# Hybrid encoder block on one core: another order of the splits of x, of the rotations and of the key loads in the in-projection

## The chip, the core and the metric

The kernel runs on one core of a Trainium2 chip. A core has TensorE (PE, matrix products into PSUM), VectorE (DVE), ScalarE (ACT), GpSimd (POOL) and SyncE (SP, which here only issues transfers), and 16 DMA engines between the device's memory and the core's on-chip memory. Each engine works through its own instructions in order; an instruction that has to wait holds up everything behind it on its engine. A transfer is issued by SP, ACT or POOL, in that engine's order, and lands later.

The metric is the time of one execution in microseconds (us) on the device. A profile shows one execution, with its span from the first to the last instruction.

## The reference

One transformer layer for a prompt of 512 tokens and a sample of 256 tokens (768 rows together), width 2048, all in float32:

```python
h = rmsnorm(x, ln_mix_g)
z = h @ w_in                      # 2048 -> 1024 Fourier | 1024 q | 256 k | 256 v
of = fourier_mix(z[..., :1024])   # 8 groups x 128 channels: Re(2-D DFT), then a 128x128 map
q, k = apply_rope(q), apply_rope(k)
oa = window_attention(q, k, v, sink)   # 16 heads, 4 key heads, +-128 positions
x = x + concat(rmsnorm(of), rmsnorm(oa)) @ w_out
x = x + relu(rmsnorm(x) @ w_up) ** 2 @ w_down
return rmsnorm(x)
```

## The kernel before

Every matrix product is made of three: each operand is split into a high part (a rounded copy, made by ScalarE) and a low part (the remainder, made by VectorE), and high x high, high x low and low x high are summed. So each weight tile and each tile of x costs one ScalarE and one VectorE instruction before TensorE can use it. The line numbers are those of the profile.

The stages in question come one after the other on TensorE:

1. **V** (L543): the value columns, chunk by chunk; x arrives transposed.
2. **Products** (`product7`, L287): six sets of columns (three column pairs, two halves of the contraction) times seven products, 42 steps, with sums of blocks of x and of the weights so that seven products serve for eight (the names a11, s1, s2, s3, a22, s4, a12). Step n issues product n on TensorE, the low part of the weights of product n+2 (L273), the sums and high part of product n+3 (L257, L265), and the load of product n+5 (L238). Two tables, `high_at` and `low_at`, say at which step a block of x is subtracted (L404), and its high (L407) and low (L410) part made; `k_at` says the same for the rotation of the keys. Beside them, rows of x are loaded again through POOL's queue (`row_load`, L613), squared by ScalarE (`row_square`, L617), summed to the row norms, transposed by TensorE (L625) into a PSUM buffer, copied by ScalarE (`row_spread`, L629, tile `rb`) and spread over the partitions. The PSUM buffer is one of two that the products also take.
3. **Pieces** (L970): twelve pieces, four for each of three pairs of query columns (pairs 2, 3 and 4), 48 matmuls each. Between them, at half and whole pieces, run the eight Fourier groups (`weights`, `fold`, `fold_parts`, `stage1`, `stage2`, `stage2_put`) and the rotations of the query pairs 1, 2 and 3, each in three thirds of 256 positions: `cross` on POOL (L336), `turned` on VectorE (L340, L342), a high part on ScalarE (L351), a low part on VectorE (L352), both stored by ScalarE's queue. What runs when is kept in a table, `todo`: key 8.5 is the middle of piece 9, key 9 its end. `piece_split` makes the two parts of the weights of a later piece; `piece_load` loads them through SP. Behind the last piece the same calls load and split the first weights of the out-projection.
4. **Out-projection and attention** (L1210, L1011): 24 slots of the out-projection, with the attention's matmuls strewn in between by a list of events in units of an eighth of a slot. The first slot needs the first Fourier rows (`load_of`, `split_of`, L1193), the first four weight pieces, queries and keys.

The order is fixed by hand: TensorE's throughout, that of SP, ACT and VectorE in the products, and those and POOL's from the pieces on; only POOL's order among the products is left to a planner that goes by its own costs.

On-chip memory is used again and again. A pool of tiles takes the place of one that was closed, and a new tile waits only for those older tiles whose place it takes. So the order in which tiles are first named in a pool decides whom they wait for; the kernel names some tiles (`name="z7"`) only to fix that order. The pool `xp` of the V stage (weights `raw`, x parts `vt`, six half-rows `xt`) gives way to `hq` of the products (tags z10, z01, d7, wr, then ws and z11), and that to `fp` of the Fourier groups. The query side has pools from the other end of the memory: `kp` (rotation) and `kq` (mask, sink, keys `kd`, queries `qs`, first Fourier rows `ofr`); `kq` can only open when `fp` is closed, at key 9.

Of the kernel before, what the change touches and what calls it, by code (L numbers as in the profile page):

```python
# [20 lines left out]
P = 128  # L21
# [19 lines left out]
def hybrid_encoder(ctx: ExitStack, tc: tile.TileContext, a: dict):  # L41
# [157 lines left out]
    with ExitStack() as ph:  # L199
# [235 lines left out]
        def first_split(e):  # L435
            for i in range(4):
                k = 4 * e + i
                split(fx["h11"][:, k], fx["l11"][:, k], fx["d"][:, i], g0[:, k : k + 1])
# [6 lines left out]
        for e in range(2):  # L445
# [5 lines left out]
            step(low_at, 12 + 2 * e, lambda e=e: difference(e))  # L451
            step(high_at, 13 + 2 * e, lambda e=e: xhigh(h1, fx["d"], e))
            step(low_at, 13 + 2 * e, lambda e=e: xlow(l1, fx["d"], h1, e))
            step(low_at, 16 + e, lambda e=e: xsum(b11, b21, b11, e))
            step(high_at, 18 + e, lambda e=e: xhigh(h0, b11, e))
            step(low_at, 19 + e, lambda e=e: xlow(l0, b11, h0, e))
            step(high_at, 24 + e, lambda e=e: xhigh(h1, b22, e))
            step(low_at, 24 + e, lambda e=e: xlow(l1, b22, h1, e))
            if e == 0:
                step(high_at, 26, second_block)  # L460
# [4 lines left out]
        step(low_at, 33, first_block)  # L465
        step(low_at, 27, lambda: first_load(0))
        for e in range(2):
            step(low_at, 33 + 4 * e, lambda e=e: first_split(e))
            if e == 0:
                step(low_at, 33, lambda: first_load(1))  # L470
# [183 lines left out]
        with tc.tile_pool(name="hq", bufs=1, reuse_waits="tile") as hq["p"], tc.manual_schedule(  # L654
            engines={mybir.EngineType.SP, mybir.EngineType.Activation, mybir.EngineType.DVE}
        ):
            for tag, shape, bufs in (("z10", [P, HALF], 3), ("z01", [P, HALF], NS7), ("d7", [P, 4, HALF], 1), ("wr", [P, 4, 256], 3)):
                hq["p"].tile(shape, F32, tag=tag, name="z7", bufs=bufs)
# [7 lines left out]
            step(k_at, 28, k_tables)  # L666
            step(k_at, 33, k_loads)
            step(k_at, 34, k_scale)
            step(k_at, 34, k_keep)
            for n in range(NP7):  # L670
# [16 lines left out]
                if n in (18, 20, 22, 24):  # L687
                    for i in range(3 * n // 2 - 15, 3 * n // 2 - 12):
                        row_square(i)
                if n in (16, 18, 20, 22):  # L690
                    for i in range(3 * n // 2 - 12, 3 * n // 2 - 9):
                        row_load(i)
                if n in (33, 34, 35):
                    back7(n - 33)
                if n == 24:
                    row_norms()
# [10 lines left out]
            for n in range(NP7, NP7 + 2):  # L707
                for fn in k_at.get(n, ()):
                    fn()
# [4 lines left out]
        fctx = ExitStack()  # L714
        fp = fctx.enter_context(tc.tile_pool(name="fp", bufs=1, reuse_waits="tile"))
        cc = fp.tile([P, 2, P], F32, tag="cc", name="cc")
# [8 lines left out]
        for tag, w, bufs in (("wf", P, 2), ("zf", T, 2), ("fe", 320, 1), ("fo", 256, 1)):  # L725
            fp.tile([P, w], F32, tag=tag, name="z7", bufs=bufs)
        fp.tile([P, 2, 2, P], F32R, tag="cw", name="cw", bufs=2)
        for tag in ("ah", "al"):
            fp.tile([P, T], F32, tag=tag, name="z7")
        tabh = fp.tile([P, 4, 256], F32R, tag="tabh", name="tabh")  # L730
        tabl = fp.tile([P, 4, 256], F32R, tag="tabl", name="tabl")


        def weights(g):
            wf = fst[g].pop("w")
            pc = pp.tile([P, 512], F32, tag="f", bufs=4, name="pc")
            cw = fst[g]["cw"] = fp.tile([P, 2, 2, P], F32R, tag="cw", name="cw", bufs=2)
# [27 lines left out]
        def fold_parts(g):  # L765
            sh = fst[g]["sh"] = fp.tile([P, 6, P], F32R, tag="sh", name="sh")
            sl = fst[g]["sl"] = fp.tile([P, 6, P], F32R, tag="sl", name="sl")
            split(sh[:], sl[:], fst[g].pop("s")[:])

        def stage1(g, b):  # L770
            if b == 0:
                for x in ("ah", "al"):
                    fst[g][x] = fp.tile([P, 6, P], F32R, tag=x, name=x)
            sh, sl, cw, ah, al = (fst[g][x] for x in ("sh", "sl", "cw", "ah", "al"))
            pa = pp.tile([P, 512], F32, tag="f", bufs=4, name="pa")
            if b == 0:
# [4 lines left out]
                t = fp.tile([P, 2, P], F32, tag="ft", name="ft")  # L781
# [21 lines left out]
        def stage2(g):  # L803
# [7 lines left out]
            of = fp.tile([P, T], F32, tag="of", name="of")  # L811
# [7 lines left out]
            else:  # L819
                sq = fst[g + 2 if g + 2 < FG else g]["z"]  # L820
# [26 lines left out]
        def open_attention():  # L847
            open_pool("kq", ("mask", [P, 384], a["c_mask"]), ("sink", [P, 64], a["attn_sink"].partition_broadcast(P)))
            kt["kd"] = kt["kq"].tile([P, NKV, T], F32R, tag="kd", name="kd")
            for u in range(3):  # L850
# [27 lines left out]
        def load_k():  # L878
            nc.sync.dma_start(f32(kt["kd"][:]), kr_d[:].rearrange("(p h) t -> p h t", h=NKV))

# [3 lines left out]
        def q_tile(u):  # L884
            state[u] = {"qs": kt["kq"].tile([P, 2, 4, P], F32R, tag="qs", name="qs", bufs=3)}
# [13 lines left out]
        def after(piece, fn):  # L899
            todo.setdefault(piece, []).append(fn)  # L900
# [3 lines left out]
        def turn(pair, s, t):  # L904
            turned(pair, s)
            parts(pair, s, lambda dt, fn: todo.setdefault(t + dt, []).insert(0, fn), (0.5, 1))
# [3 lines left out]

        def close_fourier():
            fctx.close()
            open_attention()
            load_k()

        turns = [(1, s, t) for s, t in enumerate((1, 3, 5))] + [(2, s, t) for s, t in enumerate((7, 8, 8.5))] + [(3, s, t) for s, t in enumerate((9, 9.5, 10))]
        for g in range(FG + 2):
            if g < FG:
                after(g - 0.5, lambda g=g: (weights(g), fold(g)))
            if g >= 2:  # L920
                after(g - 0.5, lambda g=g: stage2(g - 2))
            if 1 <= g <= FG:
                after(g - 0.5, lambda g=g: (stage1(g - 1, 0), stage1(g - 1, 1)))
                after(g, lambda g=g: stage1(g - 1, 2))
            if g < FG:
                after(g, lambda g=g: fold_parts(g))
            if g >= 2:
                after(g, lambda g=g: stage2_put(g - 2))
            if g + 2 < FG:
                after(g, lambda g=g: load_group(g + 2))  # L930
        for pair, s, t in turns:
            after(t - 0.5, lambda pair=pair, s=s: cross(pair, s))
            after(t, lambda pair=pair, s=s, t=t: turn(pair, s, t))
        after(9, close_fourier)
        after(9.5, fourier_norm)
        after(9.5, lambda: load_q(0))
        after(9.5, lambda: load_of(0, [kt["kq"].tile([P, 4, P], F32, tag="ofr", name="ofr", bufs=2) for _ in range(2)]))
        after(9.5, lambda: load_q(2))
        after(10.5, negate_sink)
        after(10.5, lambda: load_q(1))  # L940
# [4 lines left out]
        tabs = [fp.tile([P, T], F32, tag=t, name="tab")[:, :512].rearrange("p (k t) -> p k t", k=2) for t in ("ah", "al")]  # L945
# [1044 lines left out]
```

## Time and profile before

| | |
|---|---|
| three runs | 2588.67, 2588.93, 2590.66 us; median 2588.93 |
| the profiled execution | 2589.08 us, span 2587.3 us |
| mean granted TensorE clock | 0.995 |
| V stage on TensorE | to 40.7 us |
| products | 40.7 to 225.5 us |
| pieces | 225.5 to about 364 us |
| first out-projection matmul | 377.06 us |
| MLP and end | from about 730 us to the end |

In the rows of the profile, a time in us since the span's start comes first, then a duration, the engine, the line of the kernel, the operation, written tile <- read tiles, the shape; in brackets how long the engine sat idle before and what ended that. The list of waits has engine, line and what it waited for, then us in total, times, longest. The rows of transfers have their size and the us from issue to landing. "xN" stands for N instructions put into one row, or N in a group.

### The profile page before, as it was taken

The page shows a single profiled execution, that of the slowest core. Times are in us where ns is not written, and L with a number is a line of the kernel's source. Part 1 is how long each engine was busy: PE and PEld are TensorE (multiplying, and loading weights), DVE is VectorE, ACT ScalarE, POOL GpSimd, SP SyncE. Part 2 cuts the span into 40 slices and gives each one's busy share as a digit, 9 for nine tenths or more (in the row PEclk, how much of TensorE's full clock was granted, in tenths as well). Part 3 has the DMA queues.
Part 4 walks back from the last instruction along what each step waited for, and adds up shares of the span by engine and source line. Part 5 has one row for each costly group of instructions (what it writes and reads, how often), then busy time and mean ns, then how long its engine had stood idle before and what let it go on. Part 6 is the DMA issues. An engine that isn't in the chain of part 4 may idle for free.

```text
span 2587.3 us, 34692 instructions
## 1 busy us (share of the span) xinstructions
PE 2558.9 (99%) x13415; PEld 2341.8 (91%) x13415; DVE 1809.0 (70%) x2152; ACT 1125.9 (44%) x1622; POOL 266.8 (10%) x385
## 2 busy tenths in 40 slices
PE   9999989999999999999999999999999999999998
PEld 9989978888899999999999999988888888888887
DVE  7776757777555656555877877667776765777687
ACT  7353537774333333333444554433333333333335
POOL 0022332232201011000000000110000000000000
PEclk9999989999999999999999999999999999999999
DMA  8576367555654445456666666775543662555264
GB/s 300 201 263 222 121 193 218 149 151 193 225 190 157 163 160 188 159 190 237 213 214 232 231 214 208 245 305 176 184 155 110 218 233 82 179 179 164 97 208 155
DMA packets 260724, 496.99 MB, mean 192 GB/s; under 512 B 21098, under 2 KB 145520, under 8 KB 260304
## 3 DMA queue, kind: packets, MB, share of 16 engines
q1 hardware_dynamic: 190816, 328.20, 39.6%
q10 hardware_dynamic: 54000, 105.75, 10.9%
q0 software_dynamic: 15744, 60.83, 6.9%
q8 instruction: 105, 1.72, 0.3%
q14 instruction: 59, 0.48, 0.1%
HBM read 373.19 MB, written 121.51 MB: 191 GB/s over the span
## 4 chain that ended last, share of the span: by engine, by line
PE 94%; issue 2%; DVE 2%; ACT 1%; DMA 1%; POOL 0%; ACTq 0%; SPq 0%; DVEq 0%; POOLq 0%
PE pu L1357 36%; PE pd L1792 35%; PE pm L1210 10%; PE p L287 4%; PE pz L970 3%; PE pv L543 1%; PE s L1011 1%; PE o L1088 1%; PE t L1066 1%; PE ptx L138 0%; PE pa L789 0%; PE pe L810 0%; PE pm L1212 0%; DMA d<-in_x_sample 0%; ACT xs L407 0%
## 5 line engine op out<-in xcount | busy, mean ns | idle before, releaser
L1357 PE MATMUL pu<-xf,wh 128*128 128x384 f32 x3072 | 780.3, 334 | 0.0
L1357 PEld LDWEIGHTS pu<-xf,wh 128*128 128x128 f32 x3072 | 554.0, 188 | 1.5 <-ACT o L1375 1.3
L1792 PE MATMUL pd<-wh,sh 128*128 128x512 f32 x1332 | 517.7, 389 | 0.0
L1792 PE MATMUL pd<-wl,sh 128*128 128x512 f32 x1332 | 517.7, 389 | 0.0
L1792 PE MATMUL pd<-wh,sl 128*128 128x512 f32 x1332 | 517.5, 389 | 0.0
L1357 PE MATMUL pu<-xf,wl 128*128 128x384 f32 x1536 | 513.1, 334 | 0.0
L1769 ACT ACTIVATE wh<-rd 128x1024 fp32r<-128x1024 f32 x200 | 202.4, 1054 | 522.2 <-PE pd L1792 416.9
L1779 DVE TENSOR_TENSOR wl<-rd,wh 128x1024 fp32r<-128x1024 f32 x200 | 236.2, 1222 | 226.1 <-ACT wh L1769 225.4
L1337 ACT ACTIVATE wh<-ur 128x1024 fp32r<-128x1024 f32 x160 | 170.1, 1063 | 382.5 <-PE pu L1357 214.2
L1792 PEld LDWEIGHTS pd<-wh,sl 128*128 128x128 f32 x1332 | 249.9, 188 | 52.1 <-DVE sl L1780 0.3
L1792 PEld LDWEIGHTS pd<-wl,sh 128*128 128x128 f32 x1332 | 250.0, 188 | 51.9
L1792 PEld LDWEIGHTS pd<-wh,sh 128*128 128x128 f32 x1332 | 250.0, 188 | 51.6
L1357 PEld LDWEIGHTS pu<-xf,wl 128*128 128x128 f32 x1536 | 288.3, 188 | 0.0
L1343 DVE TENSOR_TENSOR wl<-ur,wh 128x1024 fp32r<-128x1024 f32 x160 | 195.6, 1223 | 76.1 <-ACT wh L1337 76.0
L1378 DVE TENSOR_TENSOR o<-pu,o 128x768 f32<-128x768 f32 x160 | 153.0, 956 | 122.2 <-PE pu L1357 114.7
L287 PE MATMUL p<-xs,wh 128*128 128x384 f32 x672 | 172.8, 338 | 5.2 <-ACT rb L629 5.2
L1762 DVE TENSOR_TENSOR rd<-rd 128x1024 f32<-128x1024 f32 x112 | 131.9, 1220 | 0.0
L1357 PE MATMUL pu<-xs,wh 128*128 128x384 f32 x512 | 129.9, 334 | 0.0
L287 PEld LDWEIGHTS p<-xs,wh 128*128 128x128 f32 x672 | 122.8, 190 | 5.6 <-ACT rb L629 5.5
L1337 ACT ACTIVATE wh<-sx 128x1024 fp32r<-128x1024 f32 x64 | 67.9, 1062 | 130.5 <-PE pu L1357 99.4
L287 PE MATMUL p<-xs,wl 128*128 128x384 f32 x336 | 113.7, 338 | 0.9 <-DVE wl L273 0.7
L1780 DVE TENSOR_TENSOR sl<-sr,sh 128x768 fp32r<-128x768 f32 x111 | 105.7, 952 | 0.0
(306 smaller groups left out, 3771.6 us busy)
## 6 DMA issues: line engine op xcount, KB each, us to landing
rd<-in_w_down SPq DMA_DIRECT2D x176, 512.0 KB, 5.1
ur<-in_w_up SPq DMA_DIRECT2D x128, 512.0 KB, 3.9
sr<-sd SPq DMA_DIRECT2D x95, 384.0 KB, 5.2
pd<-o ACTq DMA_DIRECT2D x60, 384.0 KB, 2.3
o<-pd POOLq DMA_DIRECT2D x60, 384.0 KB, 6.3
sd<-sm ACTq DMA_DIRECT2D x60, 384.0 KB, 2.8
raw<-in_w_in SPq DMA_DIRECT2D x40, 512.0 KB, 4.9
raw<-in_w_out SPq DMA_DIRECT2D x32, 512.0 KB, 4.7
```

The lines of the kernel that those rows point to most:

```text
L287: nc.tensor.matmul(ps7[own, g, r][:, :HALF], l[:, i, r * P : (r + 1) * P], x[:, o, 4 * e + i, :], start=(opens and e == 0 and i == 0 and q ...
L970: nc.tensor.matmul(ps[c][s][:, :HALF], w[:, i, cs], whole[j // 2][s][o][:, 4 * (j % 2) + i, :], start=first and n == 0, stop=stop and n == 2,)
L1210: nc.tensor.matmul(ps, l(k), w[:, k % 2, :], start=(k == 0 and n == 0), stop=(k == 7 and n == 2))
L1337: nc.scalar.activation(wh[:], raw[:], AF.Copy)
L1343: nc.vector.tensor_tensor(out=wl[:], in0=raw[:], in1=f32(wh[:]), op=ALU.subtract)
L1357: nc.tensor.matmul(ps[:, t, :HALF], w[:, i, t * P : (t + 1) * P], xb[:, o, i, :], start=(s == first_of[bank] and i == 0 and n == 0), stop= ...
L1378: nc.vector.tensor_tensor(out=o, in0=src, in1=o, op=ALU.add)
L1762: add = lambda x, y, op: nc.vector.tensor_tensor(out=x[:], in0=x[:], in1=y[:], op=op)
L1769: nc.scalar.activation(wh[:], t[:], AF.Copy)
L1779: nc.vector.tensor_tensor(out=wl[:], in0=t[:], in1=f32(wh[:]), op=ALU.subtract)
L1780: nc.vector.tensor_tensor(out=sl[:], in0=sr[:], in1=f32(sh[:]), op=ALU.subtract)
L1792: nc.tensor.matmul(o, l[:, q, ts], w[:, ns], start=(j == j0 and (q, t) == (0, 0)), stop=(j == j1 and (q, t) == (1, 2)),)
```

## The change

The arithmetic is the same. What changes is when and where it is done:

- **Products.** The second half of the difference d and the sums of blocks b11 and b21 stand one to five steps later, the splits of the last blocks at other steps; `first_split(1)` falls into two halves (steps 38 and 39). The rows of x are loaded at steps 18, 19, 21, 23 (before: 16, 18, 20, 22) and squared at 19, 21, 23, 26 (before: 18, 20, 22, 24); the norms follow at 26 (before: 24). The rotation of k moves one step back, its scaling two.
- **Tiles of the products.** `hq` is laid out as ws, d7, z10, z01, wr (then z11).
- **Fourier pools.** `fp` is divided: `fb` holds what the groups need to their end (ah, al, tables, sh, sl, ft, of, cw), `fp` only the folding (fo, fe, cc, wf, zf, fs). `fp` is closed at key 7.5, and the mask, the sinks and the keys (four transfers instead of one) are loaded there; `fb` at 8.5, and queries follow. The last group's squares go into the place of sh.
- **Order at a key.** Each entry of `todo` gets a place, and the entries of a key run by place. A third of a rotation (`rotate`) is spread over a piece and a half: cross at t-0.5, turned at t, high part at t+0.5 behind the weights of the Fourier group, low part there too, store at t+1. Thirds stand at 1, 2, 3 (pair 1), 5, 6, 7 (pair 2), 8, 9, 10 (pair 3); before: 1, 3, 5; 7, 8, 8.5; 9, 9.5, 10.
- **Loads and splits around the end.** From piece 8 on, `piece_split` stands ahead of the piece's matmuls instead of in its middle; the third out-projection split moves from the last piece to the attention's events (-1.5). The Fourier norm moves from 9.5 to 10, the Fourier rows' load from 9.5 to 9, the queries' from 9.5 and 10.5 to 8.5 and 9. The two tables `c_pos` are loaded by POOL's queue instead of SP's.

The diff, cut to its core:

```diff
-            step(low_at, 12 + 2 * e, lambda e=e: difference(e))
-            step(high_at, 13 + 2 * e, lambda e=e: xhigh(h1, fx["d"], e))
-            step(low_at, 13 + 2 * e, lambda e=e: xlow(l1, fx["d"], h1, e))
-            step(low_at, 16 + e, lambda e=e: xsum(b11, b21, b11, e))
-            step(high_at, 18 + e, lambda e=e: xhigh(h0, b11, e))
-            step(low_at, 19 + e, lambda e=e: xlow(l0, b11, h0, e))
+            step(low_at, 12 + 3 * e, lambda e=e: difference(e))
+            step(high_at, 13 + 3 * e, lambda e=e: xhigh(h1, fx["d"], e))
+            step(low_at, 13 + 4 * e, lambda e=e: xlow(l1, fx["d"], h1, e))
+            step(low_at, 19 + 2 * e, lambda e=e: xsum(b11, b21, b11, e))
+            step(high_at, 20 + 2 * e, lambda e=e: xhigh(h0, b11, e))
+            step(low_at, 22 + e, lambda e=e: xlow(l0, b11, h0, e))
...
-            step(high_at, 26 + e, lambda e=e: xhigh(fx["h12"], b12, e))
-            step(low_at, 26 + e, lambda e=e: xlow(fx["l12"], b12, fx["h12"], e))
-            step(high_at, 29 + e, lambda e=e: xhigh(h0, b21, e))
-            step(low_at, 30 + 2 * e, lambda e=e: xlow(l0, b21, h0, e))
+            step(high_at, 28 + 5 * e, lambda e=e: xhigh(fx["h12"], b12, e))
+            step(low_at, 28 + 5 * e, lambda e=e: xlow(fx["l12"], b12, fx["h12"], e))
+            step(high_at, 29 + 2 * e, lambda e=e: xhigh(h0, b21, e))
+            step(low_at, 29 + 5 * e, lambda e=e: xlow(l0, b21, h0, e))
...
-            for tag, shape, bufs in (("z10", [P, HALF], 3), ("z01", [P, HALF], NS7), ("d7", [P, 4, HALF], 1), ("wr", [P, 4, 256], 3)):
+            for tag, shape, bufs in (("ws", [P, 4, 256], NS7), ("d7", [P, 4, HALF], 1), ("z10", [P, HALF], 3), ("z01", [P, HALF], NS7), ("wr", [P, 4, 256], 3)):
...
-            for s, n in enumerate((36, 38, 40)):
+            loads_at, squares_at = {18: 12, 19: 15, 21: 18, 23: 21}, {19: 12, 21: 15, 23: 18, 26: 21}
+            for s, n in enumerate((37, 39, 41)):
...
-        fctx = ExitStack()
+        fctx, fctx2 = ExitStack(), ExitStack()
+        fb = fctx2.enter_context(tc.tile_pool(name="fb", bufs=1, reuse_waits="tile"))
...
-                sq = fst[g + 2 if g + 2 < FG else g]["z"]
+                sq = fst[g + 2 if g + 2 < FG else g]["z"] if g < 7 else fb.tile([P, T], F32, tag="sh", name="sq")
...
+        def open_keys():
             open_pool("kq", ("mask", [P, 384], a["c_mask"]), ("sink", [P, 64], a["attn_sink"].partition_broadcast(P)))
             kt["kd"] = kt["kq"].tile([P, NKV, T], F32R, tag="kd", name="kd")
+            for g in range(NKV):
+                nc.sync.dma_start(f32(kt["kd"][:, g]), kr_d[:].rearrange("(p h) t -> p h t", h=NKV)[:, g])
...
+        def rotate(pair, s, t):
+            then = {}
+            after(t - 0.5, lambda: cross(pair, s), 3.5)
+            after(t, lambda: turned(pair, s), 4)
+            after(t + 0.5, lambda: parts(pair, s, lambda dt, fn: then.update({dt: fn}), (0, 1)), 1)
+            after(t + 0.5, lambda: then[0](), 3)
+            after(t + 1, lambda: then[1](), 5)
...
+        for g in range(FG):
+            after(g - 0.5, lambda g=g: weights(g), 0)
+            after(g - 0.5, lambda g=g: fold(g), 2)
+            after(g, lambda g=g: fold_parts(g), 1)
             if g >= 2:
+                after(g - 2, lambda g=g: load_group(g), 3)
+            for b in range(3):
+                after(g + 0.5 + b // 2 / 2, lambda g=g, b=b: stage1(g, b), 5 if b < 2 else 0)
+            after(g + 1.5, lambda g=g: stage2(g), 4)
+            after(g + 2 if g < FG - 1 else g + 1.5, lambda g=g: stage2_put(g), 2 if g < FG - 1 else 6)
+        for pair, t in ((1, 1), (2, 5), (3, 8)):
+            for s in range(3):
+                rotate(pair, s, t + s)
+        after(7.5, close_folds, 7)
+        after(8.5, close_fourier, 7)
+        after(9, lambda: load_of(0, [...]), 7)
+        after(9, lambda: load_q(1), 8)
+        after(9, negate_sink, 8)
+        after(10, fourier_norm, 0)
...
-            nc.sync.dma_start(tab, a["c_pos"][:, 2 * i : 2 * i + 2, :])
+            nc.gpsimd.dma_start(tab, a["c_pos"][:, 2 * i : 2 * i + 2, :])
...
+            if piece >= FG:
+                piece_split(piece + 2)
...
+    at(-1.5, lambda: out_split(2, False))
     at(t_w3, lambda: out_split(3, False))
```

`close_folds` closes `fp` and calls `open_keys`; `close_fourier` closes `fb`, opens the queries' pool and loads the queries of units 0 and 2.

More of the change, by code (lines that the diff above doesn't have):

```diff
@@ L433, in first_load, with first_split @@
             nc.gpsimd.dma_start(fx["d"], a["x_t"][:, 0, 4 * e : 4 * e + 4, :])
-        def first_split(e):
-            for i in range(4):
+        def first_split(e, slices):
+            for i in slices:
                 k = 4 * e + i
@@ L706, in hybrid_encoder @@
             stores7()
-            for n in range(NP7, NP7 + 2):
+            for n in range(NP7, NP7 + 3):
                 for fn in k_at.get(n, ()):
@@ L723, in load_group @@
             fst[g] = {"w": wf, "z": z}
[L725 to L731, printed above, removed]
         def weights(g):
@@ L897, in hybrid_encoder, with after, run @@
         todo = {}
-        def after(piece, fn):
-            todo.setdefault(piece, []).append(fn)
-        order = [None, 2, 0, 1, 3]
-        def turn(pair, s, t):
-            turned(pair, s)
-            parts(pair, s, lambda dt, fn: todo.setdefault(t + dt, []).insert(0, fn), (0.5, 1))
+        def after(piece, fn, place=6):
+            todo.setdefault(piece, []).append((place, len(todo[piece]), fn))
+        def run(piece):
+            for _, _, fn in sorted(todo.pop(piece, ())):
+                fn()
@@ L931, in hybrid_encoder @@
[L931 to L940, printed above, removed]
+            fctx2.close()
```

103 lines of the change are left out of this document (50 added, 53 removed).

## The prediction

> **What bounds the kernel now.** I read the busy shares first, then what TensorE waited for, each under its heading row.
>
> ```profile
> span 2587.3 us, 34692 instructions
> PE 2558.9 (99%) x13415; PEld 2341.8 (91%) x13415; DVE 1809.0 (70%) x2152; ACT 1125.9 (44%) x1622; POOL 266.8 (10%) x385
> ...
> PE pm L1210 <- ACT ofh L1193: 10.1, 1, 10.1
> PE p L287 <- ACT rb L629: 5.2, 1, 5.2
> PE s L1011 <- DMA ofr<-ofd: 2.2, 1, 2.2
> ...
> PE pa L789 <- DVE cw L70: 0.9, 2, 0.6
> PE p L287 <- DVE wl L273: 0.7, 2, 0.5
> ```
>
> TensorE is the bound: it is idle for 2587.3 - 2558.9 = 28.4 us in all. The diff leaves its matmuls as they are, so it can only win idle time, and slow matmuls after idle time. These five waits, 19.1 us, lie between the first product and the out-projection, where the diff works. The next view is TensorE in order of time around the two large ones.
>
> ```profile
> 162.37 0.27 PE L625 MATMUL pr<-ident,r 128*6 128x128 f32 x1
> ...
> 174.92 1.01 PE L287 MATMUL p<-xs,wh 128*128 128x384 f32 x2 [5.19 <-ACT rb L629]
> ...
> 177.00 0.84 PE L287 MATMUL p<-xs,wh 128*128 128x384 f32 x2
> ...
> 177.96 0.84 PE L287 MATMUL p<-xs,wh 128*128 128x384 f32 x2
> ...
> 180.76 0.51 PE L287 MATMUL p<-xs,wh 128*128 128x384 f32 x2
> ...
> 181.28 0.51 PE L287 MATMUL p<-xs,wh 128*128 128x384 f32 x2
> ...
> 341.93 0.86 PE L970 MATMUL pz<-xf,wh 128*128 128x384 f32 x4
> ...
> 363.73 0.51 PE L970 MATMUL pz<-xs,wl 128*128 128x384 f32 x2
> 366.43 0.51 PE L1011 MATMUL s<-kd,qs 128*128 128x256 f32 x2 [2.19 <-DMA ofr<-ofd]
> 377.06 0.80 PE L1210 MATMUL pm<-wh,ofh 128*128 128x512 f32 x1 [10.13 <-ACT ofh L1193]
> 377.66 0.63 PE L1210 MATMUL pm<-wl,ofh 128*128 128x512 f32 x1
> 378.08 0.63 PE L1210 MATMUL pm<-wh,ofh 128*128 128x512 f32 x1
> ...
> 382.67 0.40 PE L1210 MATMUL pm<-wh,ofh 128*128 128x512 f32 x1
> 382.90 0.40 PE L1210 MATMUL pm<-wl,ofh 128*128 128x512 f32 x1
> ```
>
> Each stall costs more than itself. After the first, three matmuls take 0.96 us (177.00 to 177.96) where they later take 0.52; eighteen ran so from 174.92 to 180.76, that is 5.84 - 6 x 0.52 = 2.7 us lost. After the second a matmul starts every 0.42 us (377.66 to 378.08) until about 382.4, later every 0.23; 5.3 us at some 0.55 of the speed lose 2.3 us. So the rb stall is worth 5.2 + 2.7 = 7.9 us and the start of the out-projection 2.2 + 10.1 + 2.3 = 14.6 us. With the 0.7 and 0.9 the most that can be won is **24.1 us**. The causes stand on ScalarE (first five rows) and on SyncE's queue (last three):
>
> ```profile
> 150.38 0.63 ACT L617 ACTIVATE d<-d 128x512 f32<-128x512 f32 x1 [1.42 <-DMA d<-in_x_sample]
> 172.29 1.06 ACT L265 ACTIVATE wh<-wr 128x1024 fp32r<-128x1024 f32 x1 [2.05 <-DVE wr L257]
> 173.26 1.47 ACT L407 ACTIVATE xs<-xr 128x1536 fp32r<-128x1536 f32 x1
> 174.63 0.24 ACT L629 COPY rb<-pr 6x128 f32<-6x128 f32 x1
> ...
> 375.44 1.06 ACT L69 ACTIVATE wh<-raw 128x1024 fp32r<-128x1024 f32 x1 [7.72 <-DMA raw<-in_w_out]
> ...
> 351.83 0.33 SPq L879 DMA_DIRECT2D kd<-k  x1
> ...
> 361.70 0.52 SPq L895 DMA_DIRECT2D qs<-ql  x1
> ...
> 370.01 0.55 SPq L79 DMA_DIRECT2D raw<-in_w_out  x1
> ```
>
> ScalarE waits for rows of x in its squares (1.42 us here, and in the round before it); VectorE and ScalarE then feed each other late, and the copy of rb, which frees the PSUM buffer that product 30 opens second, comes at 174.63. At the end, ScalarE sits 7.72 us in front of an out-projection weight that SyncE issued at 370.01, and the Fourier split that TensorE needs stands behind it. SyncE was late because keys, queries and Fourier copies were all loaded after piece 9.
>
> **The change part by part.**
>
> *Products.* A product has 24 matmuls, 8 x 0.52 = 4.16 us. The squares move from steps 18, 20, 22, 24 to 19, 21, 23, 26, with loads at 18, 19, 21, 23, so that data has one to three steps (4.2 to 12.5 us). The subtractions of x and their splits, 1.7 us of VectorE each by this row's form,
>
> ```profile
> 130.07 1.75 DVE L410 TENSOR_TENSOR xs<-xr,xs 128x1536 fp32r<-128x1536 f32 x1
> ```
>
> no longer stand in consecutive steps 14 to 20: there VectorE had weight split, weight sum, PSUM sum and one of these, 1.1 + 1.1 + 0.5 + 1.7 = 4.4 us in a 4.16 us step; now every second step is 2.7. So VectorE should keep a lead of some 3 us, and ScalarE should reach the squares after their data. What remains for rb: the transposed norms end at 162.64; the second half of product 30 opens at 162.64 + 1.5 x 4.16 = 168.9. Before it, ScalarE copies product 27's first half at 156.4 and has wh 30 at 157.9; VectorE's low part and next sum (1.1 each) end at 160.2; wh 31 and the high part of a block (1.06 + 1.47) at 162.7; its low part, wl 31 and sum 32 (1.7 + 1.1 + 1.1) at 166.7. Behind that ScalarE has 1.06 + 1.47 + 0.24 (the rows at 172.29 to 174.63, started back to back), so rb ends at about 169.4. I leave **0.5 us**; the ends are 0 and the old 7.9. The 0.7 behind wl goes, being lag of the same engines. If the cover fails (the 1.7 us parts late), products 19 or 25 wait instead, a microsecond each.
>
> The new order of the tiles in this stage has a price. The weight tiles wr lay over V's operands vt; now they lie behind 11136 words of other tiles, over the fourth to sixth x half-rows, which ScalarE is still squaring.
>
> ```profile
> 42.21 1.05 ACT L555 ACTIVATE xt<-xt 128x1024 f32<-128x1024 f32 x1
> ...
> 44.87 1.06 ACT L265 ACTIVATE wh<-wr 128x1024 fp32r<-128x1024 f32 x1 [0.49 <-DMA wr<-in_w_in]
> ...
> 40.88 0.33 SPq L238 DMA_DIRECT2D wr<-in_w_in  x1
> ...
> 45.97 1.23 DVE L273 TENSOR_TENSOR wl<-wr,wh 128x1024 fp32r<-128x1024 f32 x1 [4.19 <-ACT wh L265]
> ...
> 49.02 0.51 PE L287 MATMUL p<-xs,wh 128*128 128x384 f32 x2
> ```
>
> The load can go at 43.4 (the square at 42.21 and its read-out) instead of 40.88, 2.5 us later; landing 4.0 us on, its split ends at 43.4 + 4.0 + 1.06 + 1.23 = 49.7, and product 2 (49.02) needs it in its third matmul, at 49.4. I take **0.5 us** lost; ends 0 and 6 (a landing of 9.7, the slowest of that batch).
>
> *Pieces 0 to 7.* The same Fourier matmuls run in the same order. The tables go to POOL's queue, behind the last turn of k and the last stores; they are needed a piece later. A third of a rotation now runs per piece (pair 1 at 1 to 3, pair 2 at 5 to 7, pair 3 at 8 to 10, before 1, 3, 5; 7, 8, 8.5; 9, 9.5, 10), turned after a piece, its high part behind the next weights copy. That copy (cw) was late behind a rotation's high part twice; I take the **0.9** back whole; ends 0 and 0.9. A piece's third costs VectorE 0.7 + 0.8 + 0.7 us, beside matmuls that never waited for VectorE in a stretch that already holds one:
>
> ```profile
> 320.00:330.00 10.00, 10.00 (x69) 10.00 (x67) 6.99 (x14) 5.53 (x12) 5.81 (x4) 1.00 0.28 94
> ```
>
> (Busy us in 10 of TensorE, weight loads, VectorE, ScalarE and POOL.)
>
> *Pieces 8 to 11 and the hand-over.* The weight splits go ahead of each piece's matmuls, so the raw tiles come free half a piece (4 us) sooner; the third out-projection split leaves the last piece for the attention's start. The keys, now four transfers, load at 7.5 over the folding tiles: the first waits for POOL's square of group 6. Behind them on SyncE stand one weight load, then the queries for units 0 and 2. These take the place of the folds' tiles and wait for group 7's squares on POOL, whose end the row of before shows 4.5 us behind its last Fourier matmul (341.93).
>
> ```profile
> 344.56 1.90 POOL L822 TENSOR_TENSOR ssf<-ssf,zf 128x768 f32<-128x768 f32 x1
> ```
>
> In the shifted time of this trace, 7.9 + 0.7 + 0.9 - 0.5 - 0.5 = 8.5 us earlier, that matmul ends at 333.4, so the queries go at 338; group 7's copy lands some 2 us later; the Fourier copies (eight issues of 0.5 to 0.6 us on) go at 342 to 343 and land by 348 if they take 5 us; the third weight goes at 346, the fourth, after its split, at 350 and lands at 355. TensorE leaves the last piece at 364.1 - 8.5 = 355.6. ScalarE reaches the Fourier split at about 353, two microseconds ahead. The stall then has no cause left. What is late next is VectorE: it does the last two copies of pair 4, the Fourier low part and two weight low parts in the first 5 us, without the 2.3 us that the slow matmuls had given it, and the fourth weight's low part and the first softmax rows come within half a microsecond of their use. I leave **1.5 us** of the 14.6; ends 0 and 14.6.
>
> *Sum.* Won 7.9 + 0.7 + 0.9 + 14.6 = 24.1; left or added 0.5 + 0.5 + 1.5 = 2.5; net 21.6. Against the profiled execution, 2589.1 us (span 2587.3), that is 2567.5; the runs' median lies 0.2 below it, which I neglect. All later stages follow TensorE, with no wait of it in the list, and move as a whole.
>
> **The rivals.**
>
> *The hand-over stalls in part.* If SyncE is held 8 us more before the Fourier copies or the last weights, TensorE waits 5 to 8 us and runs slow for 2: 2575 to 2578. For: ten transfers in a row behind POOL. Against: 5 us of margin at 348.
>
> *rb stays late.* 2567.5 + 7.4 = 2575, if the x rows arrive late through POOL's queue again.
>
> *Nothing moves where it matters*, the same two waits standing behind other instructions: 2588 to 2589. Against it speaks that the keys' 1.5 MB, landing from 351.83 on, are really gone from the congested place.
>
> *Slower: ScalarE's stores in transfer slots.* At 361.70 SyncE's load was held by a store it doesn't read:
>
> ```profile
> SPq L895 <- DMA qh<-zh: 7.9, 1, 7.9
> ...
> ql<-zs ACTq DMA_DIRECT2D x1, 256.0 KB, 9.2
> ```
>
> So issues seem to wait for the landing of an earlier one across both queues. ScalarE now has five query stores after 338 with twelve loads between, in its own order ahead of the Fourier split. If each waits a round trip d, the split ends at 338 + 5d + 1.1. At d = 9.2 that is 385.1, a stall of 29.5 + 2.3 us in place of 14.6, less the other 8.5: 2589.1 + 8.7 = 2598. It is slower by over 0.2% from d = 8.5. Against: 9.2 was measured while the keys landed.
>
> *Slower: POOL shuts VectorE out.* In the row from 320 to 330 VectorE and POOL are busy for 6.99 + 5.81 = 12.8 us of 10. If nothing of the two could overlap, each piece with a third would stretch by 28%; the twelve pieces last from 225.5 to 364.1, 11.6 us each,
>
> ```profile
> L970 PE MATMUL pz<-xf,wh x192: 333/334/417, 225.5 to 345.6; 128*128 128x384 f32 x192
> ```
>
> so nine pieces lose 9 x 11.6 x 0.28 = 29 us: 2567.5 + 29 = 2597. It decides once VectorE's work and the part of POOL's that shuts it out fill a piece. TensorE at 10.00 of 10 in that row, with a third in it, speaks against. [...]
>
> **How the numbers follow.** Forecast (2564 to 2572) 0.68; hand-over in part 0.12; rb late 0.07; nothing 0.06; slower 0.07 (stores 0.05, ports 0.02). From no change a measurement here tells 0.2%, 5.2 us. Faster: 0.68 + 0.12 + 0.07 = 0.87; same 0.06; slower 0.07. The range runs from 2564 (all 24.1 us won, and 1 more) to 2581, over the two partial cases; it leaves out 0.13 above and a little below.
>
> **What would show it.** Right: in the list of TensorE's waits, rb under 1.5 us and the Fourier split under 3; matmul spacing 0.23 from the first out-projection matmul; a short new wait at product 2 near 49.4; first out-projection matmul at about 356. Wrong: a wait over 3 us for rb, for a weight or for the Fourier split; ScalarE's stores issued at 8 us distance; new VectorE waits in the pieces.

## The result and the profile after

The changed kernel takes 2568.68 us (median of four runs, 2567.70 to 2568.78) against 2588.80 for the kernel before (four runs): 20.1 us less, ratio 0.992 with a 95% interval of 0.9903 to 0.9937. The forecast was 2567.5, faster; it holds to 1.2 us. Two executions far slower than all others, one of the kernel before (3534.79 us) and one of the kernel with the weights half a piece sooner (5195.10 us), are left out of every median and ratio here. The profiled execution took 2568.73 us. Its span and busy line, and its list of waits of TensorE (us in total, times, longest):

```profile
span 2567.0 us, 34696 instructions
PE 2553.6 (99%) x13415; PEld 2337.0 (91%) x13415; DVE 1816.2 (71%) x2152; ACT 1125.4 (44%) x1622; POOL 268.1 (10%) x387
```

```profile
PE pa L793 <- DVE cw L70: 2.0, 3, 1.2
...
PE pm L1223 <- DVE wl L70: 1.0, 2, 0.5
PE p L287 <- ACT rb L629: 0.6, 1, 0.6
...
PE s L1024 <- DVE es L1044: 0.3, 1, 0.3
```

Idle time fell from 28.4 to 13.4 us, and the same 13415 matmuls are busy 5.3 us less (2558.9 to 2553.6): 15.0 + 5.3 = 20.3 us, the whole difference of the spans. The two large waits have shrunk to 0.6 and 1.3 us; one has grown, that for the split of a Fourier group's channel weights (`cw`), from 0.9 to 2.0. TensorE in order of time at both places, by the changed kernel's line numbers (L986 was L970, L1024 was L1011, L1223 was L1210):

```profile
168.67 0.62 PE L287 MATMUL p<-xs,wh 128*128 128x384 f32 x2 [0.60 <-ACT rb L629]
...
356.98 0.40 PE L1024 MATMUL s<-kd,qs 128*128 128x256 f32 x2
357.21 0.40 PE L1223 MATMUL pm<-wh,ofh 128*128 128x512 f32 x1
357.44 0.40 PE L1223 MATMUL pm<-wl,ofh 128*128 128x512 f32 x1
...
361.33 0.50 PE L1223 MATMUL pm<-wl,ofh 128*128 128x512 f32 x1 [0.50 <-DVE wl L70]
```

In the out-projection a matmul follows every 0.23 us from the first on: the slow matmuls are gone with the stall. SyncE (first five rows) and ScalarE (last three) ahead of the out-projection:

```profile
330.50 1.75 SPq L855 DMA_DIRECT2D kd<-k  x4
334.75 0.38 SPq L79 DMA_DIRECT2D raw<-in_w_out  x1
340.92 0.61 SPq L901 DMA_DIRECT2D qs<-qh  x1
...
347.01 1.21 SPq L189 DMA_DIRECT2D ofr<-ofd  x2
...
350.91 1.06 SPq L79 DMA_DIRECT2D raw<-in_w_out  x2
```

```profile
354.99 0.59 ACTq L346 DMA_DIRECT2D ql<-zs  x1
355.63 1.15 ACT L1206 ACTIVATE ofh<-ofr 128x512 fp32r<-128x512 f32 x2 [1.40 <-DVE zs L352]
357.56 1.06 ACT L69 ACTIVATE wh<-raw 128x1024 fp32r<-128x1024 f32 x1 [0.78 <-DMA raw<-in_w_out]
```

The Fourier rows are issued at 347.0, 10 us ahead of TensorE's end with the pieces; before, at 363.6 of 364.1, half a microsecond ahead of it.

### The profile page after: what moved, and what is told of

It reads as the page before. It is cut to its first block, busy times and chain, and to the rows that moved or that the text cites. A ratio compares the mean times of both kernels' runs of the same rounds, so it can differ in the third digit from the quotient of the medians.

```text
span 2567.0 us, 34696 instructions
## 1 busy us (share of the span) xinstructions
PE 2553.6 (99%) x13415; PEld 2337.0 (91%) x13415; DVE 1816.2 (71%) x2152; ACT 1125.4 (44%) x1622; POOL 268.1 (10%) x387
## 4 chain that ended last, share of the span: by engine, by line
PE 95%; DVE 3%; ACT 1%; issue 1%; DMA 0%; ACTq 0%; SPq 0%; DVEq 0%; POOLq 0%; POOL 0%
PE pu L1371 36%; PE pd L1806 35%; PE pm L1223 10%; PE p L287 6%; PE pz L986 2%; PE pv L543 1%; PE o L1101 1%; PE s L1024 1%; PE t L1079 1%; PE ptx L138 0%; DVE al L70 0%; DVE wl L70 0%; DVE fs L753 0%; DVE zf L749 0%; ACT wh L69 0%
```

## The experiments

Each kernel's median stands beside that of the kernel before on the same chip; the ratio has its 95% interval. "After" is the changed kernel, whose difference is -20.1. An interval reaches 2 to 5 us to each side, so a difference of that size between two rows rests on the traces too.

| Kernel | us | before | difference | ratio |
|---|---|---|---|---|
| before + products' steps | 2581.8 | 2589.7 | -7.9 | 0.9958 to 0.9982 |
| after, products' steps old | 2577.3 | 2589.7 | -12.4 | 0.9935 to 0.9967 |
| after, rows of x old | 2573.2 | 2589.7 | -16.4 | 0.9918 to 0.9954 |
| after, parts of x old | 2576.3 | 2589.7 | -13.4 | 0.9933 to 0.9964 |
| before + third split moved | 2589.5 | 2589.5 | 0.0 | 0.9989 to 1.0007 |
| after, keys late | 2570.6 | 2589.5 | -18.9 | 0.9914 to 0.9944 |
| after, third split back | 2569.2 | 2589.5 | -20.3 | 0.9908 to 0.9935 |
| after, weights half a piece sooner | 2566.8 | 2589.5 | -22.7 | 0.9899 to 0.9926 |
| the same, queries of unit 1 later | 2567.6 | 2589.0 | -21.4 | 0.9905 to 0.9934 |
| after, thirds old | 2574.0 | 2589.0 | -15.0 | 0.9926 to 0.9959 |
| before + thirds new | 2587.4 | 2589.0 | -1.6 | 0.9985 to 1.0004 |
| before + splits ahead | 2584.5 | 2589.0 | -4.5 | 0.9973 to 0.9992 |

### The two halves of the change

All of the diff's edits to the steps of the products, put into the kernel before (without the new tile order), and the same edits taken out of the changed kernel:

```diff
+            step(low_at, 12 + 3 * e, lambda e=e: difference(e))
...
+            loads_at, squares_at = {18: 12, 19: 15, 21: 18, 23: 21}, {19: 12, 21: 15, 23: 18, 26: 21}
```

> The kernel before, with the changed steps of the products alone (parts of x, rows of x, rotation of k); the products' tile order, the pieces and the loads around the last pieces stay. Theory (the stall at the rb copy and the one at the out-projection are independent, and the first is made in the products): rb wait 0.3 to 1.0 us in place of 5.2, pieces begin at 217.3 to 218.3 us, the wait for the Fourier split stays at 9 to 11 us, time 2588.8 - 7.9 - 0.7 = 2580.2, at least 2579 and at most 2582. Rival (what is won early is given back at the out-projection, because the late transfers there don't follow TensorE): pieces begin at 217.5, but the wait for the Fourier split grows by up to 8 us: 2585 to 2589.

> The changed kernel with the old steps of the products (parts of x, rows of x, rotation of k). Theory: rb waits 5 us again and 2.7 us go in slow matmuls, all else as in the changed kernel: 2568.7 + 7.4 = 2576.1, between 2575 and 2577.5. Rival (the rb stall came from the old tile order of the products, which is the changed one here): rb waits under 1.5 us, 2568.5 to 2570.

The first won 7.9 us, with an rb wait of 1.0 and the old 10.4 and 2.2 at the out-projection; without the products' steps the rest won 12.4, with the old rb wait of 5.2 and only 1.0 (wl) at the out-projection. Together 20.3, where the whole is 20.1: the two halves are independent, and each rival (a gain given back later; the new tile order as the cure of rb) falls.

### Rows of x or parts of x

```diff
-            loads_at, squares_at = {18: 12, 19: 15, 21: 18, 23: 21}, {19: 12, 21: 15, 23: 18, 26: 21}
+            loads_at, squares_at = {17: 12, 18: 15, 20: 18, 22: 21}, {18: 12, 20: 15, 22: 18, 24: 21}
```

> The changed kernel with the rows of x near their old steps: squares at 18, 20, 22, 24 and norms at 24 as before, loads at 17, 18, 20, 22 (the first a step later than before, since its tile is now read until step 17). Theory V (rb was late because VectorE had parts of x in consecutive steps): rb wait at most 1.5 us, 2568.5 to 2570.5. Theory R (rb was late because ScalarE waited for rows of x in its squares): the squares wait 4 us or more for data in all, rb waits 3 to 5 us, 2573 to 2576.5.

The other kernel keeps the new rows and puts the parts of x back (`difference` at 12 and 14, its low part at 13 and 15, sums at 16 and 17, and so on).

> The changed kernel with the parts of x at their old steps, the rows of x and the rotation of k at the new ones. Theory V (VectorE's consecutive parts of x made rb late): rb wait 3 to 5 us, 2573 to 2576.5. Theory R (the rows of x did): rb wait at most 1.5 us, 2568.5 to 2570.5. If both give a part, each of the two kernels loses some and the two losses make about 7.4 us together.

Measured: 3.7 us of the gain lost with the old rows, 6.7 with the old parts, where 7.7 went with both. Neither theory is the whole: each edit alone leaves most of the stall standing, and the two losses add up to 10.4 us, not to the 7.4 expected if they were shares of it. ScalarE with the old rows, then with the old parts:

```profile
126.47 0.63 ACT L617 ACTIVATE d<-d 128x512 f32<-128x512 f32 x1 [2.15 <-DMA d<-in_x_prompt]
...
142.37 0.63 ACT L617 ACTIVATE d<-d 128x512 f32<-128x512 f32 x1 [1.64 <-DMA d<-in_x_sample]
...
172.12 0.24 ACT L629 COPY rb<-pr 6x128 f32<-6x128 f32 x1
```

```profile
132.40 0.61 ACT L617 ACTIVATE d<-d 128x512 f32<-128x512 f32 x1
...
140.51 0.63 ACT L617 ACTIVATE d<-d 128x512 f32<-128x512 f32 x1 [4.04 <-DMA d<-in_x_prompt]
...
173.55 0.24 ACT L629 COPY rb<-pr 6x128 f32<-6x128 f32 x1
```

With the old rows the squares wait 7.0 us for data in all (2.8 in the changed kernel), because ScalarE came to three of the four batches 3.3 to 4.2 us after the batch's first load was issued, and these rows took 4.7 to 6.9 us to land. With the old parts VectorE's lag brings ScalarE to the first squares 4.6 us later (132.4 against 127.8); the next rows go into the same places, so their loads go later too, and the squares wait 6.5 us again. Both roads end at the same copy.

The rows of VectorE name a piece of its lag that the prediction didn't have. Before, then after:

```profile
112.81 1.76 DVE L410 TENSOR_TENSOR xs<-d,xs 128x1536 fp32r<-128x1536 f32 x1 [2.58 <-ACT xs L407]
```

```profile
118.21 1.75 DVE L410 TENSOR_TENSOR xs<-d,xs 128x1536 fp32r<-128x1536 f32 x1
```

A low part in the step of its high part waits 2.58 us for ScalarE; this one, a step later, waits for nothing. The first half of d stays in the step of its high part, and there VectorE still waits 2.58 us (at 101.32 in both kernels).

### The third out-projection split

Put behind the Fourier split in the kernel before, and back into the last piece in the changed kernel:

```diff
-            if piece == n_in - 1:
-                piece_split(piece + 3)
...
+    at(-1.5, lambda: out_split(2, False))
```

> The kernel before with one edit: the third out-projection split leaves the end of the last piece and stands behind the first Fourier split, at -1.5, as in the changed kernel. Theory (the weight is late because SyncE issues it at 370, so it only waits elsewhere): the Fourier split runs at about 367.5, the first out-projection matmul at 369, some 8 us sooner; then TensorE stops for the third weight, issued at 370.0 and split at 376 to 378, after 12 to 14 matmuls. Won: those matmuls, 12 x 0.42 = 5 us at most; 2583 to 2587. Rival (the order of the two splits on ScalarE was the whole fault): no second wait, 8 us or more won, 2578 to 2581.

> The changed kernel with the third out-projection split back at the end of the last piece. Theory (with the weight landed at 357.5 the order of the two splits is worth only the time by which it lands behind the Fourier rows): ScalarE splits the weight at 357.6, the Fourier rows at 358.6, the first out-projection matmul comes at 359.8 in place of 357.2, and the waits for that weight's low part, 1.0 us, go: 1 to 3 us lost, 2569.5 to 2571.5. Rival (this order was the main cause of the old stall): a wait for the Fourier split of 8 us or more, 2577 and up.

Alone it wins nothing: the first out-projection matmul came at 367.94, 9 us sooner, and then TensorE stopped for the weight (3.3 us) and stayed slow. The expected gain of up to 5 us was too much. In the changed kernel the edit is worth less than a run can tell (2569.2 against 2568.7; waits of 1.0 us for the Fourier split and 0.6 us for queries in place of 1.0 for wl and 0.3 for es). What ScalarE finds waiting matters, not the order of its two splits.

### The keys

```diff
+        def load_k():
+            nc.sync.dma_start(f32(kt["kd"][:]), kr_d[:].rearrange("(p h) t -> p h t", h=NKV))
...
+        after(9, load_k, 6.5)
```

> The changed kernel with the keys in one transfer at key 9 again, between the queries of units 0 and 2 and the Fourier rows; all else stays. Theory (1.5 MB of keys in that place delay what SyncE issues behind them by the 8 to 9 us that their landing takes): Fourier rows issued at 355 in place of 347, third and fourth weight at 359 and later, TensorE waits 5 to 9 us for the Fourier split and runs slow for 2 us: 2575 to 2580. Rival (the keys' place doesn't matter, the earlier weight splits and the third split behind the Fourier split make the gain): wait under 1.5 us, 2568.5 to 2570.5.

1.2 us lost: the theory, which was also my argument against "nothing moves", falls. The keys went at 345.49, and loads behind them were held, but the Fourier rows had already slipped through right behind the keys (346.06), and the queries of two units stood ahead of them. Only the last two weights came late; TensorE waited 2.0 us for them. The 1.2 us are less than the two intervals can tell apart, but they are not the 5 us and more of the theory. This is not the old order in full: there four queries came between the keys and the Fourier rows.

### The thirds of the rotations

The old keys and the old grouping (high part at once behind the turn) in the changed kernel; then only the new keys in the kernel before:

```diff
+        for pair, ts in ((1, (1, 3, 5)), (2, (7, 8, 8.5)), (3, (9, 9.5, 10))):
+            for s, t in enumerate(ts):
+                after(t - 0.5, lambda pair=pair, s=s: cross(pair, s))
+                after(t, lambda pair=pair, s=s, t=t: turn(pair, s, t))
```

> The changed kernel with the thirds of the rotations at their old keys and in their old order (1, 3, 5; 7, 8, 8.5; 9, 9.5, 10; high part at once behind the turn), the queries of unit 1 at key 10 for that. All else stays: keys early, weight splits ahead from piece 8, third split behind the Fourier rows. Theory C (five thirds within two pieces make ScalarE wait for VectorE and POOL, the weight splits stand behind them, and SyncE's weight loads behind the splits): SyncE's second out-projection weight is issued at 338 or later in place of 334.8, the queries at 343 or later, TensorE waits 1 to 6 us at the out-projection: 2570 to 2576. Rival (splits ahead of the piece or the freed folding tiles are what matters): the same waits as in the changed kernel, 2568 to 2569.7.

```diff
+        turns = [(pair, s, t + s) for pair, t in ((1, 1), (2, 5), (3, 8)) for s in range(3)]
```

> The kernel before with one edit: the thirds at 1, 2, 3; 5, 6, 7; 8, 9, 10. Theory C: ScalarE reaches the weight split that was at 347.9 six or more us sooner, and SyncE comes past it (before: 350.2) by as much; the keys and all behind then wait only for the Fourier tiles, which POOL frees at 346.5. The group moves 4 us, the stall goes from 10 to 6 us: 2582 to 2586. If the Fourier tiles were never in the way, the whole stall goes: 2575 to 2578. Rival (thirds don't matter): 2588 to 2590.

With the old thirds the changed kernel loses 5.1 us, the most of any single part of the second half. ScalarE:

```profile
355.93 0.63 ACT L351 ACTIVATE zh<-zs 128x512 fp32r<-128x512 f32 x1 [3.25 <-DVE zs L342]
...
357.01 1.06 ACT L69 ACTIVATE wh<-raw 128x1024 fp32r<-128x1024 f32 x1 [0.44 <-ACT zh L351]
...
360.40 1.15 ACT L1203 ACTIVATE ofh<-ofr 128x512 fp32r<-128x512 f32 x2 [1.59 <-DVE zs L992]
```

This is theory C on ScalarE: the last weight split stands behind a high part that waits 3.25 us for VectorE and comes at 357.01 (in the changed kernel at 344.75). Behind it stand a pair's copies and two stores, and so the Fourier split comes at 360.40 in place of 355.63. TensorE then waits 4.4 us in place of 1.3 and is busy 3.0 us longer. On SyncE the theory fits less well: the second weight (336.63) and the queries (342.77) are later by 2 us, less than expected. The last weight, at 361.18 in place of some 351.5, stands behind queries of unit 1, which had to move with the thirds and were held until 359.26 by a store. So the 5.1 us are those of the thirds and of this move together.

The new keys of the thirds alone, in the kernel before, halve the stall and lose it elsewhere; the 1.6 us won lie outside both expected ranges, and the interval includes no change:

```profile
PE pm L1210 <- ACT ofh L1193: 6.2, 1, 6.2
...
PE pa L789 <- DVE cw L70: 4.9, 4, 1.5
```

At the out-projection 12.3 us become 6.2; but with the high parts still ahead of the cw copies, cw waits 4.9 us in place of 0.9. The changed kernel pays 2.0 for the same thirds. That its new order at a key makes the difference is the likely reading; no run changes that order alone.

### Weight splits ahead of the piece

```diff
+            if piece >= FG:
+                piece_split(piece + 2)
             wh, wl = in_w.pop(piece)
```

> The kernel before with one edit: from piece 8 on the weight splits stand ahead of the piece's matmuls. Theory S (the raw weight tiles, freed half a piece sooner, are what lets SyncE go ahead): SyncE's weight load that waited 14.6 us for a low part is issued at 344 or earlier in place of 350.2, bounded by the Fourier tiles at 346.5, and later weights come 4 us sooner: 2583 to 2587. Theory C (the splits then still stand behind the thirds of key 8 on ScalarE): less than 2 us won, 2587 to 2590.

4.5 us won, with SyncE's weight at 343.58 in place of 350.20, as theory S had it. Of the parts of the second half that were tried alone in the kernel before, it won most. The waits at the out-projection are 3.3 + 0.8 + 0.5 + 0.3 = 4.9 us, and TensorE still runs slow behind them.

### Beyond the change: the wait for cw

```diff
-            after(g - 0.5, lambda g=g: weights(g), 0)
+            after(max(g - 1, -0.5), lambda g=g: weights(g), 0.5)
```

> The changed kernel with the product of a Fourier group's channel weights half a piece sooner (after a piece, behind the third block of the group before, in place of the middle of the next piece). Its PSUM buffer is the one that the second block of stage 1 takes four tiles later, so with the split half a piece ahead nothing should wait for it. Theory (the 2.0 us of waits for cw are that buffer): they go, and the time is 2566.7, 2566 to 2567.5. Rival (the copy and the low part only move in front of the fold and make ScalarE or VectorE late elsewhere): as much is lost for sh, al or zs, 2568.5 to 2571.

```diff
-        after(9, lambda: load_q(1), 8)
+        after(10.5, lambda: load_q(1), 8)
```

> The changed kernel with two edits: the channel weights half a piece sooner, and the queries of unit 1 loaded behind the last two out-projection weights on SyncE (key 10.5) in place of ahead of them (key 9). Theory (the third weight is late by the four query loads, 2.6 us of issues, ahead of it): raw weights issued at 348.3, landed by 355, the wait for their low part (1.0 us in the changed kernel) goes, and with the 2.0 us of cw the time is 2565.7 to 2566.7. Rival (VectorE, not the landing, is late there, since copies, Fourier low parts, weight low parts and softmax rows meet in 5 us): wl or the softmax's es still waits 1 us or more, 2567 to 2568.

The first takes cw out of the list, as its theory said:

```profile
PE s L1024 <- DVE es L1044: 0.9, 1, 0.9
PE p L287 <- ACT rb L629: 0.7, 1, 0.7
PE pm L1223 <- DVE wl L70: 0.6, 1, 0.6
```

The first out-projection matmul comes at 354.85 in place of 357.21. The median is 1.8 us lower (2566.84 against 2568.68), less than the two intervals can tell apart, so that it beats the changed kernel is shown at its place in the trace and not in the time. The second edit issues the last weights from 346.62 on, and wl still waits 1.0 us; the time is no better (2567.64). So its rival holds: VectorE, not the landing, is late there. ScalarE (first row) makes both high parts from 354.17 on, but VectorE comes to the low part only behind the Fourier low parts:

```profile
354.17 1.99 ACT L69 ACTIVATE wh<-raw 128x1024 fp32r<-128x1024 f32 x2
```

```profile
355.65 2.20 DVE L1207 TENSOR_TENSOR ofl<-ofr,ofh 128x512 fp32r<-128x512 f32 x2
357.77 1.75 DVE L70 TENSOR_TENSOR wl<-raw,wh 128x1024 fp32r<-128x1024 f32 x1
```

## Why the prediction was right, and where not

- **rb.** Right, in size too: 0.6 us left (0.5 predicted), rb done at 168.6 (169.4). The working named the rows and the parts of x, and both are needed: the old rows alone bring back a wait of 3.7 us, the old parts alone one of 4.0. It missed VectorE's 2.58 us waits for high parts of the same step.
- **Product 2.** 0.5 us was charged, nothing was lost. The load waited for one square fewer than I had laid out:

```profile
42.32 0.33 SPq L238 DMA_DIRECT2D wr<-in_w_in  x1
```

  It is 1.1 us sooner than the 43.4 predicted, and product 2 starts at 49.00 without a wait.
- **cw: the step that failed.** "I take the 0.9 back whole"; it grew to 2.0, a sum 2.0 us too low, and the bounds 0 and 0.9 left a loss out. I had looked only at the high part that no longer stands ahead of the copy. In the changed kernel other work does (ScalarE, middle of piece 3):

```profile
255.84 0.45 ACTq L346 DMA_DIRECT2D ql<-zs  x1
256.40 0.86 ACT L995 COPY zs<-pz 128x384 f32<-128x384 f32 x2 [0.97 <-PE pz L814]
257.14 0.40 ACT L69 ACTIVATE cw<-pc 128x256 fp32r<-128x256 f32 x1
```

  Behind the scaling of a Fourier block and two stores, ScalarE comes late to a pair's copies and so to cw. In the code these PSUM buffers go round in fours: the product for cw, two of stage 2 and the first block of stage 1 take one each, and the second block takes the first again, so it waits until VectorE has read it for cw. The kernel with the weights half a piece sooner agrees: there the wait is gone.
- **Hand-over.** 1.3 us left (1.0 wl and 0.3 es) where 1.5 was kept, for the reason given: VectorE is late. SyncE's times were 3 to 5 us too early (queries at 338, measured 340.92; Fourier rows at 342 to 343, measured 347.01), and ScalarE came to the Fourier split at 355.63, not at 353. The group's copy waits on ScalarE until the store of the group before has landed, which the working had left out,

```profile
336.55 0.62 ACT L816 COPY of<-pe 128x512 f32<-128x512 f32 x1 [2.79 <-DMA ofd<-of]
```

  and POOL's squares follow it. The 5 us of margin took that up. Why the stall went was told wrongly in part: I gave the keys the weight, and undoing them costs 1.2 us. The spread thirds (5.1 us when undone) and the splits ahead of a piece (4.5 when done alone) carry more, and no part alone gives the 12.4 us of this half. The splits ahead weren't undone in the changed kernel, nor were the queries' and Fourier rows' places, the new order of the tiles in the products or the tables' queue tried alone; their shares stay open.
- **The sum.** By the after trace: rb 4.6, wl 0.7, cw -1.1, hand-over 11.0, matmuls 5.3, together 20.5. From the predicted 21.6 one comes there by cw 2.0 and rb 0.1 lower, and by product 2 0.5, the slow matmuls 0.3 (5.0 predicted) and the hand-over 0.2 higher. So part of the closeness is luck: terms that were 2.1 us too high and 1.0 us too low make up for each other in part.
- **Slower rivals.** ScalarE's stores don't wait a trip each (the last pair goes at 354.26 and 354.99 and lands 6.6 and 7.1 us later). VectorE and POOL are busy for 12.5 us of 10 with TensorE at full:

```profile
217.20:357.00 139.80, 137.84 (x894) 137.38 (x894) 100.32 (x200) 65.19 (x157) 47.62 (x39) 1.00 0.53 173
320.00:330.00 10.00, 10.00 (x70) 10.00 (x69) 7.23 (x13) 5.01 (x10) 5.31 (x4) 1.00 0.69 220
```

  The twelve pieces take 139.8 us (138.6 before); the 1.2 are mostly cw's (1.1), not 29. Ports, as the prediction's chances name them, no run here shows; what POOL's work costs VectorE in time the runs do. In the kernel before:

```profile
320.99 1.08 DVE L70 TENSOR_TENSOR al<-ft,ah 128x256 fp32r<-128x256 f32 x1 [0.48 <-ACT ah L69]
```

```profile
320.32 1.47 POOL L821 TENSOR_TENSOR zf<-of 128x768 f32<-128x768 f32 x1 [8.84 <-DVE of L815]
```

  The same instruction of VectorE takes 0.43 us where POOL is idle (243.78). In the seven other groups it starts during such a square of POOL's, takes 0.62 to 1.08 us and ends 0.27 to 0.28 us after the square. So these seven were held up by POOL, and the busy time includes the holding; TensorE, at 10.00 of 10 in that row, lost nothing by it.

## What to carry to other kernels

Price a copy by everything that stands ahead of it on its engine after the edit, not by the one instruction that the edit takes away, and give such a term a loss among its bounds. Where a stall ends a chain through several queues, undoing one part (here 0 to 5 us) or doing one alone (0 to 4.5) doesn't show the worth of the whole (12.4), since each part only moves the queue on to the next hold. A low part should stand a step behind its high part when the engine that makes it has work queued (2.58 us a time here).

## What the runs showed that I had not expected

**A load can be held until a store that it doesn't read has landed.** In the prediction I read SyncE's hold until 361.70 as one behind ScalarE's store, and made a slower rival of it. The rival fell, but the reading holds. The store ahead of that hold, in the kernel before, and its landing (size, us from issue):

```profile
352.87 0.37 ACTq L346 DMA_DIRECT2D qh<-zh  x1
...
qh<-zh ACTq DMA_DIRECT2D x1, 256.0 KB, 8.8
```

It lands at 361.67, and the held load (`qs<-ql`, other data) goes at 361.70. The kernel before with the products' steps has the same pair:

```profile
344.84 0.37 ACTq L346 DMA_DIRECT2D qh<-zh  x1
...
353.68 0.52 SPq L896 DMA_DIRECT2D qs<-ql  x1
```

Here 8.84 us lie between the two. In the kernel with the new thirds the store goes at 355.83 and the held load at 363.11, and a high part on ScalarE that waits for such a store to land starts at 363.17; in the one with the splits ahead it is 351.29 (a Fourier store) and 358.44. SyncE's list of waits names the store: `qh<-zh` in the kernel before (7.9 us) and with the new thirds (19.4 us in two holds), `ofd<-of` with the splits ahead (10.3 us). The keys, in one transfer, land 0.7 to 2.2 us ahead of these holds' ends, and the stores beside them are long: 8.8 and 9.2 us in the kernel before, while the median store of this size took 3.0 us (`qh`) and 2.9 us (`ql`) from 325 to 375 us in the changed kernel with late keys, in which none was issued while the keys landed. There the keys themselves are what a load was held for:

```profile
345.49 0.53 SPq L856 DMA_DIRECT2D kd<-k  x1
...
353.37 0.51 SPq L902 DMA_DIRECT2D qs<-ql  x1
...
kd<-k SPq DMA_DIRECT2D x1, 1536.0 KB, 7.9
```

Other loads pass between such a transfer and the load that is held for it. Why an issue waits for a transfer that it doesn't read, no run here shows.

**Slow matmuls followed a wait of 2.1 us.** With the old thirds in the changed kernel:

```profile
361.08 0.60 PE L1220 MATMUL pm<-wh,ofh 128*128 128x512 f32 x1 [2.10 <-ACT ofh L1203]
361.49 0.63 PE L1220 MATMUL pm<-wl,ofh 128*128 128x512 f32 x1
```

0.42 us a matmul for almost 4 us, then 0.23 (366.00 to 366.23). The granted clock (the third number from the end of a row by stretches) says the same:

```profile
361.60:362.00 0.40, 0.40 (x3) 0.30 (x2) 0.40 (x2) 0.40 (x1) 0.40 (x1) 0.50 1.05 357
365.00:367.00 2.00, 2.00 (x12) 1.66 (x11) 0.41 (x4) 0.00 (x0) 0.20 (x1) 1.00 1.03 305
```

It is 0.50 in the first row and 1.00 in the second. The 2.10 us did not stand alone: TensorE had waited 0.76 us ahead of them, with two matmuls between (at 358.49). Waits of 0.96 us (third split back) and 1.2 us (cw) were not followed by slow matmuls; 1.94 and 1.26 us with two matmuls between (third split moved) were, and those of 3.3 to 10.1 us too, for 3 to 7 us. At the two stalls of the kernel before the clock stood at 0.50 for 6.8 and 13.6 us (173.8 to 180.6, 368.4 to 382.0). How long TensorE must be idle for its clock to fall, the runs don't show.
